# A hybrid decoder layer: inverse blocks by DMA, squares on ACT, pools and output rows in another order

## The chip, the cores and the metric

The kernel runs on one core of a Trainium2 chip. The metric is the time of one execution on the device in microseconds. Five engines work side by side: PE (TensorE: matrix products), DVE (VectorE), ACT (ScalarE), POOL (GpSimd) and SP (SyncE, which here issues nearly all DMAs). Each engine takes its own instructions in the order that was fixed when the program was built; semaphores hold it until what it reads is there.

## The reference

One layer on 1024 tokens of width 1024, all in float32:

- h = LN(x); z = h @ w_in (2304 columns). Of z, 1792 columns belong to time mixing with 8 heads of 64 (r, k, v and three low-rank inputs), 512 to causal pooling with windows 2, 4, 8, 16 and one 128 x 128 product per window.
- Time mixing: z is mixed with the token before it; decay = exp(-exp(-softplus(-u) - 0.5)), a function of one number per element; k is normalised per head; a recurrence over tokens keeps a 64 x 64 state per head; its output is normalised per head, scaled, shifted, gets a bonus and is multiplied by a gate.
- mix = concat(time mixing, pooling) @ w_out; h = LN(alpha h + mix).
- A SwiGLU network (width 2816) and a gated embedding of p follow, and a last LN.

## The kernel before

Products in full precision are made of three rounded ones (high x high, low x high, high x low); the high part is a cast on ACT, the low part a subtraction on DVE. `tile` names buffers in rings (`tag`, `bufs`): a buffer is given again when its last reader is done, in the order of the program text. A scheduler orders each engine's instructions when the program is built: what comes earlier in the text goes first where both could run, and `tc.high_priority()` (around `solve`) lifts a block over all else.

**Order of the work.** Until about 62 us the inputs are loaded, normalised and transposed into `hT`. Then, for a pair index p of heads (4) and a half s of the tokens (2), a tile t = 4 s + p is prepared by `fr(t)` (line 690): `z_pair` makes r, k, v for both halves (s = 0) or `z_again` loads the second half (s = 1), and `front` (line 362) turns them into the operands of the chunked recurrence. Two tiles make a pair, solved by `solve` (line 699): `gram` (line 435) forms the products gB, gK of 64-token chunks; `inverse` (line 462) inverts unit triangular 64 x 64 blocks; `chain` (line 544) walks over 8 chunks, three small products and three short DVE steps each; `post` (line 597) normalises, gates and stores a tile to `ya_d`. The loop at line 707 has `fr(t+2)`, `fr(t+3)`, `solve` of the pair t/2, four times; the pools (lines 712 to 716: `pool_group`, `pool_out`, rows to `yb_d`) follow in the text. When the last pool is done, `zpool` is closed and its memory becomes pool `s4`: `out_weights` (line 727) loads and splits w_out in 16 pieces, `mix(tt)` (line 737) loads and splits a row block of 128 tokens and makes its 2 x 24 products pm. Blocks 0 to 3 need only the first half of the tokens, and run beside the last solves; the rest comes after them. From about 645 us the second half of the layer runs.

**The steps that the change touches.** `front` computes the decay as a polynomial of degree 6 of t1 = tanh: one ACT step (line 379), five DVE steps (line 381), one ACT step into `wx` (line 385). In `inverse` the 16 x 16 diagonal blocks of gB are masked out (dg, line 472), summed to 16 columns (dc, line 474), stored to DRAM by one DMA and loaded in another arrangement, one block per partition, by a second (lines 476, 477); gB loses its diagonal blocks (line 478). After the block inversion on DVE (lines 485 to 511) `ef` holds each inverse and its transpose; one DMA stores both, one loads them back with 16 columns (cc, lines 516, 518), and DVE spreads them with the mask into E_ and F_ (line 521). Then PE multiplies: pn (gB by F_), and three rounds pzz. In `post` the reciprocal root gets one Newton step by three DVE operations (lines 607 to 609).

The queue of SP holds one DMA behind the other: one that waits for a semaphore holds those behind it.

Of the kernel before, what the change touches and what calls it, by code (L numbers as in the profile page):

```python
# [23 lines left out]
NC = 8  # L24
# [6 lines left out]
DECAY = [7.38403150e-01, -2.23932079e-01, 3.39554149e-02, -3.43247040e-03,  # L31
         2.60245296e-04, -1.58445669e-05, 7.95516283e-07]
# [10 lines left out]
def hybrid_layer(ctx, tc, x, pT, w_in, cols, rows, lora, gl, pool_w, w_out,  # L43
# [24 lines left out]
    jm = cq.tile([128, 128], F32, name="jm")  # L68
    V.tensor_scalar(jm, bones, 1.0 / 64, None, ALU.mult)
    cmat = cq.tile([128, 128], F32, name="cmat")  # L70
    V.tensor_tensor(cmat, ident, jm, ALU.subtract)
# [4 lines left out]
    for h in range(2):  # L76
        r = slice(64 * h, 64 * h + 64)
        G.affine_select(out=gmask[r, 0:64], in_=gmask[r, 0:64], pattern=[[1, 64]],
                        compare_op=ALU.is_gt, fill=0.0, base=0, channel_multiplier=-1)
        G.affine_select(out=gmask[r, 64:128], in_=gmask[r, 64:128], pattern=[[1, 64]],  # L80
                        compare_op=ALU.is_ge, fill=0.0, base=0, channel_multiplier=-1)
        G.affine_select(out=bmask[r, :], in_=bmask[r, :], pattern=[[-16, 4]],
                        compare_op=ALU.is_ge, fill=0.0, base=0, channel_multiplier=1)
        G.affine_select(out=bmask[r, :], in_=bmask[r, :], pattern=[[16, 4]],
                        compare_op=ALU.is_ge, fill=0.0, base=15, channel_multiplier=-1)
    e0 = cq.tile([128, 65 * NC + 1], F32, name="e0")
# [9 lines left out]
    qb = cq.tile([128, 2], F32, name="qb")  # L96
    V.memset(qb[:, 0:1], DECAY[5])
    V.memset(qb[:, 1:2], DECAY[0])

# [12 lines left out]
    V.tensor_scalar(oka, col[:, KA:KA + 4], -0.5, 1.0, ALU.mult, ALU.add)  # L112
    lor = cq.tile([128, 512], F32, name="lor")
# [19 lines left out]
    st1 = cp.tile([128, 2, 6], F32, name="st1")  # L133
# [50 lines left out]
    with pa:  # L184
# [74 lines left out]
        def z_mm(j):  # L259
# [102 lines left out]
        def front(pair, q, p, s, r, k, v):  # L362
# [22 lines left out]
            S.activation(wx3[:, :, 1:65], v3(pc), AF.Identity, bias=qb[:, 1:2])  # L385
# [75 lines left out]

        def inverse(pr):
# [5 lines left out]
            for q in range(2):  # L468
                A4 = gB[:, q, :, 0:64].rearrange("p c (q t) -> p c q t", q=4)
                dg = kb("dg")  # L470
                dg4 = dg.rearrange("p c (q t) -> p c q t", q=4)
                V.tensor_tensor(dg4, A4, bmask[:, None, :, None].to_broadcast([128, NC, 4, 16]), ALU.mult)
                dc = s1.tile([128, NC, 16], F32, name="dc", tag="dc", bufs=2)
# [40 lines left out]
            for q in range(2):  # L514
                d2 = dp.tile([2 * NC, 128, 16], F32, name="d2", tag="d2", bufs=4)
                nc.sync.dma_start(d2.rearrange("(x c) (a i) t -> (c a) x (i t)", x=2, i=16), ef[QR[q]])
                cc = s1.tile([128, 2 * NC, 16], F32, name="cc", tag="cc", bufs=2)
                nc.sync.dma_start(cc, d2.rearrange("g p t -> p g t"))
                E_, F_ = [s1.tile([128, NC, 64], F32, name=n, tag=n, bufs=2) for n in ("ex", "fx")]
                for i, t in ((1, F_), (0, E_)):  # L520
                    V.tensor_tensor(t.rearrange("p g (q t) -> p g q t", q=4),
                                    cc[:, NC * i:NC * i + NC, None, :].to_broadcast([128, NC, 4, 16]),
                                    bmask[:, None, :, None].to_broadcast([128, NC, 4, 16]), ALU.mult)
                EF.append((E_, F_))

# [71 lines left out]
        def post(d, py):  # L597
# [4 lines left out]
            S.activation(ys, py, AF.Square)  # L602
            pvv = chp.tile([128, 512], F32, name="pvv", tag="ch")
            mm(pvv, jm, ys, True, True)
# [6 lines left out]
            V.scalar_tensor_tensor(ys, ys, col[:, LG + p:LG + p + 1], d["bv"], ALU.mult, ALU.add)  # L611
            pg = chp.tile([128, 512], F32, name="pgate", tag="ch")
# [26 lines left out]
        def pool_group(g):  # L639
# [5 lines left out]
            pz = z_mm(14 + g)  # L645
# [75 lines left out]
        s4 = ostk.enter_context(tc.tile_pool(name="a4", bufs=2, side="right"))  # L721
        wo = act_tiles("wo")
# [4 lines left out]
        def out_weights():  # L727
            for i in range(8):
                k = OUT_K[i]
                for cf in range(2):  # L730
                    h, l = wo_part(i, cf)
                    r = s4.tile([128, 512], F32, name="wr4", tag="o", bufs=2)
# [4 lines left out]
        def mix(tt):  # L737
# [13 lines left out]
            def part(cf):  # L751
                cs = slice(512 * cf, 512 * cf + 512)
                if tt < 4:
                    o = s4.tile([128, 512], F32, name="o", tag="o", bufs=2)
# [3 lines left out]
                ps = mmp.tile([128, 512], F32, name="pm", tag="mm")  # L758
                for i in range(n):
                    wh, wl = wo_part(i, cf)  # L760
                    mm(ps, yh[i], wh, i == 0, False)
                    mm(ps, yh[i], wl, False, False)
                    mm(ps, yl[i], wh, False, i == n - 1)
                V.tensor_tensor(o, ps, o, ALU.add)  # L764
                if tt < 4:
                    nc.sync.dma_start(m_d[tsl, cs], o)
                    V.bn_stats(st1[:, cf, :], o)
            if tt >= 6:
                return yh, yl
            for cf in range(2):  # L770
                part(cf)
            if tt < 4:
                V.bn_aggr(mv1[:, tt, :], st1.rearrange("p a b -> p (a b)"))

        out_weights()
        for tt in range(4):
            mix(tt)
# [448 lines left out]
```

## Time and profile before

| | |
|---|---|
| median of 3 timed runs | 1352.28 us (1350.77 to 1353.28) |
| the profiled execution | 1357.52 us, span 1355.8 us |
| PE busy | 1309.3 us, 97% of the span |
| DVE busy | 1023.8 us, 76% |
| ACT busy | 526.9 us, 39% |
| granted TensorE clock | 0.990 of full, mean |
| DMA | 117101 packets, 173.52 MB |

Busy times are a union of the instructions' spans; matmuls are pipelined and their ends are modelled, so a busy PE can still be slower than its best. PEclk is the TensorE clock that was granted, as a share of 2.4 GHz.

### The profile page before, as it was taken

Reading aid. Unit: us, or ns where it says so; the run is one execution under the profiler, and the core shown is the slowest. Engines: PE = TensorE matmul, PEld = TensorE weight load, DVE = VectorE, ACT = ScalarE, POOL = GpSimd, SP = SyncE. Lnnn points to the kernel's source line nnn. Section 1 sums busy time; section 2 is a strip of 40 time slices with the busy share of each in tenths; the row PEclk is TensorE's granted clock in tenths of the full one; section 3 lists DMA queues with packets and bytes.
Section 4 is the critical chain, followed back from the end, with each engine's and each line's share of the span. In section 5 each row is a group of like instructions: output and inputs, shape, how many; then the busy total and the mean of one; then the engine's idle time right before and its main releaser. Section 6 shows DMA issues by size and latency. Waiting matters only on the chain.

```text
span 1355.8 us, 22923 instructions
## 1 busy us (share of the span) xinstructions
PE 1309.3 (97%) x9028; PEld 1029.2 (76%) x9028; DVE 1023.8 (76%) x1807; ACT 526.9 (39%) x889; POOL 12.8 (1%) x48
## 2 busy tenths in 40 slices
PE   6999999999997989999999999999999999999997
PEld 5787777777666667778888888888888888887886
DVE  6937566569698884556889989777766767987868
ACT  5823432244334511176434333223333334553530
POOL 0000000000000000000000000000000000000000
PEclk9999999999998999999999999999999999999999
DMA  8621130122123343263433336332323237987803
GB/s 280 216 107 51 55 75 10 59 78 55 41 58 103 91 120 93 102 215 131 150 107 117 114 113 224 116 110 102 101 79 107 101 119 261 319 282 249 264 24 124
DMA packets 117101, 173.52 MB, mean 128 GB/s; under 512 B 34688, under 2 KB 43904, under 8 KB 116992
## 3 DMA queue, kind: packets, MB, share of 16 engines
q1 hardware_dynamic: 116848, 172.01, 38.8%
q8 instruction: 71, 1.16, 0.4%
q14 instruction: 38, 0.31, 0.1%
q10 hardware_dynamic: 144, 0.04, 0.0%
HBM read 124.03 MB, written 47.97 MB: 127 GB/s over the span
## 4 chain that ended last, share of the span: by engine, by line
PE 73%; DVE 14%; DMA 8%; ACT 3%; issue 2%; SPq 0%; DVEq 0%; ACTq 0%
PE p L49 31%; PE pz L49 10%; PE pgt L49 7%; PE py L49 6%; PE pm L49 5%; PE px L49 4%; DMA ar<-a_d 2%; PE pzz L49 1%; PE pg L49 1%; PE cw L49 1%; PE cs L49 1%; DMA ab<-d 1%; DMA wdr<-ff_down 1%; DVE da L830 1%; PE cu L49 1%
## 5 line engine op out<-in xcount | busy, mean ns | idle before, releaser
L49 PE MATMUL p<-tb,p 128*128 128x512 f32 x1056 | 253.0, 395 | 0.0
L49 PEld LDWEIGHTS p<-tb,p 128*128 128x128 f32 x1056 | 198.7, 188 | 47.0
L49 PE MATMUL pz<-hT,wh 128*128 128x512 f32 x576 | 190.9, 406 | 0.0
L49 PE MATMUL p<-h,p 128*128 128x512 f32 x792 | 188.6, 392 | 0.0
L49 PEld LDWEIGHTS p<-h,p 128*128 128x128 f32 x792 | 148.7, 188 | 33.0
L829 ACT CAST p<-a 128x512 fp32r<-128x512 f32 x132 | 81.2, 622 | 181.3 <-PE p L49 138.4
L49 PEld LDWEIGHTS pz<-hT,wh 128*128 128x128 f32 x576 | 107.4, 188 | 32.9 <-issue 4.7
L49 PE MATMUL pz<-hT,wl 128*128 128x512 f32 x288 | 117.5, 408 | 0.0
L830 DVE TENSOR_TENSOR p<-a,p 128x512 fp32r<-128x512 f32 x132 | 89.3, 687 | 12.5 <-ACT p L829 12.1
L49 PE MATMUL pm<-wo,mh 128*128 128x512 f32 x224 | 78.6, 418 | 3.3 <-DVE o L764 1.4
L1001 DVE TENSOR_TENSOR u<-p,u 128x512 f32<-128x512 f32 x66 | 45.3, 687 | 31.6 <-PE p L49 31.6
L49 PEld LDWEIGHTS pz<-hT,wl 128*128 128x128 f32 x288 | 54.1, 188 | 16.5 <-issue 3.8
L49 PE MATMUL px<-da 128*128 128x512 f32 x276 | 64.3, 390 | 0.0
L49 PEld LDWEIGHTS px<-da 128*128 128x128 f32 x276 | 51.8, 188 | 10.9
L49 PEld LDWEIGHTS pm<-wo,mh 128*128 128x128 f32 x224 | 41.3, 188 | 15.8 <-ACT wo L734 1.9
L245 DVE TENSOR_TENSOR wl<-wr,wh 128x512 fp32r<-128x512 f32 x36 | 24.7, 688 | 35.1 <-ACT wh L243 34.3
L49 PE MATMUL pgt<-wg,h 128*128 128x512 f32 x192 | 48.4, 396 | 0.0
L49 PE MATMUL py<-da 128*128 128x512 f32 x204 | 47.7, 389 | 0.0
L49 PE MATMUL pm<-wo,ml 128*128 128x512 f32 x112 | 46.6, 419 | 0.0
L49 PEld LDWEIGHTS py<-da 128*128 128x128 f32 x204 | 38.3, 188 | 8.1
L243 ACT CAST wh<-wr 128x512 fp32r<-128x512 f32 x36 | 22.3, 619 | 56.3 <-PE pz L49 31.8
L1022 DVE TENSOR_TENSOR gs<-p,u 128x512 f32<-128x512 f32 x44 | 30.4, 690 | 18.1 <-PE p L49 17.3
(325 smaller groups left out, 2351.0 us busy)
## 6 DMA issues: line engine op xcount, KB each, us to landing
ar<-a_d SPq DMA_DIRECT2D x77, 256.0 KB, 4.2
wdr<-ff_down SPq DMA_DIRECT2D x55, 256.0 KB, 3.8
a<-ff_gate SPq DMA_DIRECT2D x44, 256.0 KB, 2.8
a<-ff_up SPq DMA_DIRECT2D x44, 256.0 KB, 2.8
a_d<-s SPq DMA_DIRECT2D x44, 256.0 KB, 2.3
b<-ff_down SPq DMA_DIRECT2D x22, 512.0 KB, 5.8
wr<-w_in SPq DMA_DIRECT2D x36, 256.0 KB, 2.8
a_d<-gs SPq DMA_DIRECT2D x33, 256.0 KB, 2.2
```

The lines of the kernel that those rows point to most:

```text
L49: PE.matmul(o, lhsT=l, rhs=r, start=a, stop=z)
L243: S.copy(wh, wr)
L245: V.tensor_tensor(wl, wr, wh.bitcast(F32), ALU.subtract)
L829: S.copy(h, r)
L830: V.tensor_tensor(l, r, h.bitcast(F32), ALU.subtract)
L1001: V.tensor_tensor(t, ps, u, ALU.add)
L1022: V.tensor_tensor(d, ps, u, ALU.add)
```

## The change

In `front` the polynomial is written as a product of squares: ACT makes (t1 + b0) squared, (t1 + b1) squared plus a constant, and (t1 + b2) squared; two DVE steps multiply them; ACT scales into `wx`. In `post` y0 squared is made on ACT and two DVE steps remain (the constant of the Newton step goes into the scale of the squares and `hlg`); the gate product of the last two tiles uses another PSUM bank. In `inverse` gB is stored to DRAM with rows of 64 and a pitch that makes the four diagonal blocks of a 64 x 64 matrix one strided pattern; the blocks are loaded from it. On the way back, the inverses are stored as diagonal blocks into DRAM buffers that were filled with zeros at the beginning, and E_ and F_ are loaded from these whole. gB's diagonal blocks are cleared by one multiplication with a mask. Pools are put before `fr(6)` and `fr(7)` in the text; the last pool's z products go half by half; row blocks are loaded two at a time ahead of the weights; weights come by column halves, in four buffers; the products of a part are sorted: all high x high, all low x high, all high x low. Setup lines (masks, constants) change with it and are left out here.

```diff
 front:
             pc = k2("pc")
-            S.activation(pc, t1, AF.Identity, scale=DECAY[6], bias=qb[:, 0:1])
-            for n in (0.0, DECAY[4], DECAY[3], DECAY[2], DECAY[1]):
-                V.scalar_tensor_tensor(pc, pc, n, t1, ALU.add, ALU.mult)
+            pd = k2("pd")
+            S.activation(pc, t1, AF.Square, bias=qb[:, 0:1])
+            S.activation(pd, t1, AF.Square, bias=qb[:, 1:2])
+            S.activation(pd, pd, AF.Identity, bias=qb[:, 3:4])
+            S.activation(t1, t1, AF.Square, bias=qb[:, 2:3])
+            V.scalar_tensor_tensor(pc, pc, QE[0], pd, ALU.add, ALU.mult)
+            V.scalar_tensor_tensor(pc, t1, QE[2], pc, ALU.add, ALU.mult)
...
 before inverse:
+        HS = 64 * 64 + 64
+        def rows_of(d, h):
+            return d.rearrange("(c h r) -> c h r", c=NC, h=2)[:, h, 0:64 * 64].rearrange("c (p t) -> p c t", t=64)
+        def blocks_of(d):
+            return d.rearrange("(g r) -> g r", g=64)[:, 0:1024].rearrange("g (s t) -> g s t", t=64)[:, :, 0:16]
+        d2 = [[dp.tile([2 * NC * HS], F32, name=f"d2{q}{x}", bufs=1) for x in range(2)] for q in range(2)]
+        zt = s1.tile([128, 2 * NC * HS // 128], F32, name="zt", tag="k2", bufs=KA_BUFS)
+        G.memset(zt, 0.0)
+        for q in range(2):
+            for x in range(2):
+                nc.scalar.dma_start(d2[q][x].rearrange("(p r) -> p r", p=128), zt)
 inverse:
             for q in range(2):
-                V.tensor_tensor(dg4, A4, bmask[:, None, :, None].to_broadcast([128, NC, 4, 16]), ALU.mult)
-                V.tensor_reduce(dc, dg.rearrange("p c (q t) -> p c t q", q=4), AX.X, ALU.add)
-                d1 = dp.tile([NC, 128, 16], F32, name="d1", tag="d1", bufs=4)
-                nc.sync.dma_start(d1.rearrange("c p t -> p c t"), dc)
-                nc.sync.dma_start(abf[QR[q], 0:256], d1.rearrange("c (a s) t -> (c a) (s t)", a=8))
-                V.tensor_tensor(gB[:, q, :, 0:64], gB[:, q, :, 0:64], dg, ALU.subtract)
+                d1 = dp.tile([2 * NC * HS], F32, name="d1", tag="d1", bufs=4)
+                for h, R in enumerate(HR):
+                    nc.sync.dma_start(rows_of(d1, h), gB[R, q, :, 0:64])
+                nc.sync.dma_start(abf[QR[q], 0:256].rearrange("g (s t) -> g s t", t=16), blocks_of(d1))
...
             for q in range(2):
-                nc.sync.dma_start(d2.rearrange("(x c) (a i) t -> (c a) x (i t)", x=2, i=16), ef[QR[q]])
-                nc.sync.dma_start(cc, d2.rearrange("g p t -> p g t"))
-                for i, t in ((1, F_), (0, E_)):
-                    V.tensor_tensor(t..., cc..., bmask..., ALU.mult)
+            for i in (1, 0):
+                for q in range(2):
+                    nc.sync.dma_start(blocks_of(d2[q][i]), ef[QR[q], i, :].rearrange("g (i t) -> g i t", t=16))
+                for q in range(2):
+                    for h, R in enumerate(HR):
+                        nc.sync.dma_start(EF[q][i][R], rows_of(d2[q][i], h))
+            for q in range(2):
+                V.tensor_tensor(gB[:, q, :, 0:64], gB[:, q, :, 0:64],
+                                omask[:, None, :].to_broadcast([128, NC, 64]), ALU.mult)
 post:
-            V.scalar_tensor_tensor(ys, pvv, GN_EPS, y0, ALU.add, ALU.mult)
-            V.scalar_tensor_tensor(ys, ys, -0.5, y0, ALU.mult, ALU.mult)
-            V.scalar_tensor_tensor(y0, ys, 1.5, y0, ALU.add, ALU.mult)
+            S.activation(ys, y0, AF.Square)
+            V.scalar_tensor_tensor(ys, pvv, GN_EPS, ys, ALU.add, ALU.mult)
+            V.scalar_tensor_tensor(y0, ys, 3.0, y0, ALU.subtract, ALU.mult)
...
-            pg = chp.tile([128, 512], F32, name="pgate", tag="ch")
+            pg = psa("pgate") if s and p > 1 else chp.tile([128, 512], F32, name="pgate", tag="ch")
 z_mm:
-            for q in range(2):
-                for hf in range(2):
+            for a in range(2):
+                for b in range(2):
+                    q, hf = (b, a) if by_half else (a, b)
                     z_part(pz[hf], w, q, hf)
 pool_group:
-            pz = z_mm(14 + g)
+            pz = z_mm(14 + g, g == 0)
 the loop over pairs:
+        pools = []
         for t in range(0, 8, 2):
+            for g in ({4: (3, 2, 1, 0)}).get(t, ()):
+                pools.append(pool_group(g))
+                if len(pools) > 1:
+                    pool_out(g + 1, *pools[-2])
+                if g == 0:
+                    pool_out(0, *pools[-1])
             if t < 6:
...
-        pools = [pool_group(3)]
-        for g in (2, 1, 0):
-            pools.append(pool_group(g))
-            pool_out(g + 1, *pools[-2])
-        pool_out(0, *pools[-1])
 out_weights (tags "o" get 4 buffers instead of 2, here and in mix):
-            for i in range(8):
-                k = OUT_K[i]
-                for cf in range(2):
+            for cf in range(2):
+                for i in range(8):
+                    k = OUT_K[i]
 mix, part(cf):
+                w = [wo_part(i, cf) for i in range(n)]
                 for i in range(n):
-                    wh, wl = wo_part(i, cf)
-                    mm(ps, yh[i], wh, i == 0, False)
-                    mm(ps, yh[i], wl, False, False)
-                    mm(ps, yl[i], wh, False, i == n - 1)
+                    mm(ps, yh[i], w[i][0], i == 0, False)
+                for i in range(n):
+                    mm(ps, yl[i], w[i][0], False, False)
+                for i in range(n):
+                    mm(ps, yh[i], w[i][1], False, i == n - 1)
 rows 0 to 3:
-        out_weights()
-        for tt in range(4):
-            mix(tt)
+        for t2 in (0, 2):
+            rows_ = [mix(t2), mix(t2 + 1)]
+            if t2 == 0:
+                out_weights()
+            for cf in range(2):
+                for part in rows_:
+                    part(cf)
...
```

## Rows read from the trace of the kernel before

**Rows 1.** The page's first part: busy time and share of the span of each engine.
```profile
PE 1309.3 (97%) x9028; PEld 1029.2 (76%) x9028; DVE 1023.8 (76%) x1807; ACT 526.9 (39%) x889; POOL 12.8 (1%) x48
```
**Rows 2.** Busy time by stage; last columns: granted clock, DMA share, GB/s.
```profile
core 0: us, PE busy (x) PEld busy (x) DVE busy (x) ACT busy (x) POOL busy (x), PEclk, DMA share, GB/s
0.00:41.00 41.00, 29.52 (x128) 21.98 (x129) 28.34 (x82) 26.28 (x43) 2.83 (x18) 1.00 0.86 286
...
62.00:124.00 62.00, 61.78 (x258) 47.80 (x256) 36.16 (x53) 23.43 (x40) 1.29 (x3) 1.00 0.23 85
124.00:288.00 164.00, 162.09 (x1600) 121.97 (x1600) 98.76 (x189) 54.19 (x95) 1.89 (x7) 0.98 0.19 56
288.00:415.00 127.00, 116.92 (x1516) 84.43 (x1514) 111.44 (x226) 52.00 (x87) 5.82 (x18) 0.98 0.22 56
415.00:428.00 13.00, 10.80 (x243) 10.01 (x244) 9.31 (x17) 7.16 (x11) 0.63 (x1) 0.67 0.46 118
428.00:500.00 72.00, 66.92 (x940) 47.63 (x937) 63.48 (x130) 29.29 (x54) 0.31 (x2) 1.00 0.32 93
500.00:560.00 60.00, 58.17 (x846) 43.97 (x845) 29.82 (x68) 9.26 (x22) 0.00 (x0) 1.00 0.31 87
...
645.00:1124.00 479.00, 479.00 (x2072) 388.98 (x2071) 385.96 (x611) 162.34 (x270) 0.00 (x0) 1.00 0.36 119
```
**Rows 3.** Waits of PE in 124 to 600 us: total, times, longest.
```profile
PE pn L49 <- DVE fx L521: 6.8, 4, 2.1
PE pp L49 <- issue: 3.1, 1, 3.1
...
PE pg L49 <- DVE bk L417: 1.4, 2, 0.7
...
```
**Rows 4.** Groups by line: shapes, count, busy us, mean ns, idle before.
```profile
L381 DVE SCALAR_TENSOR_TENSOR pc<-pc,t 128x512 f32<-128x512 f32 x40 | 27.4, 686 | 10.8 <-ACT pc L379 10.3
...
L474 DVE TENSOR_REDUCE dc<-dg 128x128 f32<-128x512 f32 x8 | 8.2, 1029 | 0.0
...
L379 ACT ACTIVATE pc<-t,qb 128x512 f32<-128x512 f32 x8 | 5.7, 710 | 0.0
L521 DVE TENSOR_TENSOR fx<-cc,bmask 128x512 f32<-128x512 f32 x8 | 5.5, 688 | 3.3 <-DMA cc<-d 3.3
...
L472 DVE TENSOR_TENSOR dg<-gB,bmask 128x512 f32<-128x512 f32 x8 | 5.5, 683 | 0.0
```
**Rows 5.** DVE in order of time, third pair: start us, us.
```profile
390.49 0.68 DVE L449 TENSOR_TENSOR gB<-pg,gmask 128x512 f32<-128x512 f32 x1
...
400.49 0.17 DVE L490 TENSOR_TENSOR tm<-ef,ab 128x4 f32<-128x4 f32 x1 [0.98 <-DMA ab<-d]
...
409.61 0.37 DVE L512 COPY ef<-ef 128x256 f32<-128x256 f32 x1
```
**Rows 6.** DMA issues: count, KB each, median us from issue to landing.
```profile
d<-ef SPq DMA_DIRECT2D x8, 128.0 KB, 2.4
cc<-d SPq DMA_DIRECT2D x8, 128.0 KB, 3.4
...
d<-dc SPq DMA_DIRECT2D x8, 64.0 KB, 2.4
ab<-d SPq DMA_DIRECT2D x8, 64.0 KB, 2.1
```
**Rows 7.** PE in order of time between pools and output products; in brackets: stood.
```profile
411.48 1.10 PE L49 MATMUL pp<-wsa,plw 128*128 128x512 f32 x2 [3.09 <-issue]
413.51 2.04 PE L49 MATMUL pp<-wsa,plw 128*128 128x512 f32 x2 [0.93 <-DVE wsa L673]
417.65 3.68 PE L49 MATMUL pn<-fx,gB 64*64 64x64 f32 x64 [2.10 <-DVE fx L521]
...
428.51 0.51 PE L49 MATMUL pm<-wo,mh 128*128 128x512 f32 x1
```
**Rows 8.** SP in the same stretch: issue of the first row's second half.
```profile
437.07 0.38 SPq L746 DMA_DIRECT2D mr<-ya_d  x1
```

More of the change, by code (lines that the diff above doesn't have):

```diff
@@ L29 @@
 GN_EPS = 1e-5 * 64
-DECAY = [7.38403150e-01, -2.23932079e-01, 3.39554149e-02, -3.43247040e-03,
-         2.60245296e-04, -1.58445669e-05, 7.95516283e-07]
+QB = [2.6446236909266547, -4.777402204072105, -7.825890616949517]
+QE = [148.19110777287312, 64.07475031771858, 7.586255131509925]
+QS = 7.95516283e-07
 MU, W0, A0, KK, KA, RK, LG, LB, PS, IG, IB, MG, MB = 0, 14, 18, 22, 26, 30, 34, 38, 42, 46, 54, 62, 70
@@ L67, in hybrid_layer @@
     V.memset(bones[64:128, 64:128], 1.0)
-    jm = cq.tile([128, 128], F32, name="jm")
-    V.tensor_scalar(jm, bones, 1.0 / 64, None, ALU.mult)
     cmat = cq.tile([128, 128], F32, name="cmat")
-    V.tensor_tensor(cmat, ident, jm, ALU.subtract)
+    V.scalar_tensor_tensor(cmat, bones, -1.0 / 64, ident, ALU.mult, ALU.add)
     gmask = cq.tile([128, 128], F32, name="gmask")
@@ L85, in hybrid_layer @@
                         compare_op=ALU.is_ge, fill=0.0, base=15, channel_multiplier=-1)
+    omask = cq.tile([128, 64], F32, name="omask")
+    V.tensor_scalar(omask.rearrange("p (q t) -> p q t", q=4), bmask[:, :, None].to_broadcast([128, 4, 16]),
+                    -1.0, 1.0, ALU.mult, ALU.add)
     e0 = cq.tile([128, 65 * NC + 1], F32, name="e0")
@@ L95, in hybrid_layer @@
     V.memset(epsg, GN_EPS)
-    qb = cq.tile([128, 2], F32, name="qb")
-    V.memset(qb[:, 0:1], DECAY[5])
-    V.memset(qb[:, 1:2], DECAY[0])
+    qb = cq.tile([128, 4], F32, name="qb")
+    for i, c in enumerate(QB + [QE[1]]):
+        V.memset(qb[:, i:i + 1], c)
     col = cp.tile([128, NCOL], F32, name="col")
@@ L112, in hybrid_layer @@
     V.tensor_scalar(oka, col[:, KA:KA + 4], -0.5, 1.0, ALU.mult, ALU.add)
+    hlg = cq.tile([128, 4], F32, name="hlg")
+    V.tensor_scalar(hlg, col[:, LG:LG + 4], -0.5, None, ALU.mult)
     lor = cq.tile([128, 512], F32, name="lor")
@@ L130, in hybrid_layer @@
     hT = act_tiles("hT")
-    st1 = cp.tile([128, 2, 6], F32, name="st1")
+    st1 = cp.tile([128, 4, 2, 6], F32, name="st1")
     mv1 = cp.tile([128, 4, 2], F32, name="mv1")
@@ L257, in z_part, with z_mm @@
                 mm(pz, ls[q][:, i, :], hh[:, k, :], False, k == KT - 1)
[L259 removed]
+        def z_mm(j, by_half=False):
             w = z_weights(j)
             pz = [mmp.tile([128, 512], F32, name=f"pz{hf}", tag="mm") for hf in range(2)]
[L262 to L263 removed]
+            for a in range(2):
+                for b in range(2):
+                    q, hf = (b, a) if by_half else (a, b)
                     z_part(pz[hf], w, q, hf)
@@ L384, in front @@
             wx3 = wx[:, 0:65 * NC].rearrange("p (c t) -> p c t", t=65)
-            S.activation(wx3[:, :, 1:65], v3(pc), AF.Identity, bias=qb[:, 1:2])
+            S.activation(wx3[:, :, 1:65], v3(pc), AF.Copy, scale=QS)
             Ep = s2.tile([128, NC, 65], F32, name="Ep", tag="ep", bufs=1)
@@ L721, in hybrid_layer @@
         s4 = ostk.enter_context(tc.tile_pool(name="a4", bufs=2, side="right"))
+        OB = 4
         wo = act_tiles("wo")
@@ L727, in out_weights @@
         def out_weights():
-            for i in range(8):
-                k = OUT_K[i]
-                for cf in range(2):
+            for cf in range(2):
+                for i in range(8):
+                    k = OUT_K[i]
                     h, l = wo_part(i, cf)
-                    r = s4.tile([128, 512], F32, name="wr4", tag="o", bufs=2)
+                    r = s4.tile([128, 512], F32, name="wr4", tag="o", bufs=OB)
                     nc.sync.dma_start(r, w_out[128 * k:128 * k + 128, 512 * cf:512 * cf + 512])
@@ L753, in part @@
                 if tt < 4:
-                    o = s4.tile([128, 512], F32, name="o", tag="o", bufs=2)
+                    o = s4.tile([128, 512], F32, name="o", tag="o", bufs=OB)
                     nc.sync.dma_start(o, h_d[tsl, cs])
@@ L766, in part @@
                     nc.sync.dma_start(m_d[tsl, cs], o)
-                    V.bn_stats(st1[:, cf, :], o)
+                    V.bn_stats(st1[:, tt, cf, :], o)
             if tt >= 6:
                 return yh, yl
+            if tt < 4:
+                return part
             for cf in range(2):
                 part(cf)
-            if tt < 4:
-                V.bn_aggr(mv1[:, tt, :], st1.rearrange("p a b -> p (a b)"))
-        out_weights()
-        for tt in range(4):
-            mix(tt)
+        for t2 in (0, 2):
[5 more added lines that the diff above has]
+                    part(cf)
+            for tt in (t2, t2 + 1):
+                V.bn_aggr(mv1[:, tt, :], st1[:, tt].rearrange("p a b -> p (a b)"))
     sp = ctx.enter_context(tc.tile_pool(name="b", bufs=2, reuse_waits="tile"))
```

15 lines of the change are left out of this document (3 added, 12 removed).

## The prediction

> **What bounds the kernel now.** I read the busy line of the page first: PE is busy 97% of the span, VectorE (DVE) 76% [rows 1]. The reader is to see that this is no proof of a kernel that can't get faster: it is a mean over stages. So the second view was the busy time by stage [rows 2]. From 645 to 1124 us PE is busy in every microsecond at full clock, 2072 matmuls in 479.0 us, 0.231 us each; nothing of the change is there. From 124 to 560 us, where the time mixing is solved, the rows differ: PE stands still 1.9 us in 124–288, 10.1 in 288–415, 2.2 in 415–428, 5.1 in 428–500 and 1.8 in 500–560, together 21.1 us. The granted clock of the same rows is 0.98, 0.98, 0.67, 1.00 and 1.00. With two levels, 1.2 and 2.4 GHz, that is (0.02×164 + 0.02×127 + 0.33×13)/0.5 = about 20 us at the lower one, and half of it, 10 us, is lost wherever PE had work. So 31 us can be seen to be recoverable. In 288–415 and 428–500 DVE is busy 111.4 of 127 and 63.5 of 72 us: there it nearly sets the pace; in 500–560 it is busy 29.8 of 60. The third view, the waits of PE in 124–600, says who held it: the product pn of the inverse waits for fx in each of the four pairs (6.8 us), the pooling product pp for 3.1 + 0.9 us, pg for bk 1.4 us [rows 3]. The low clock comes behind such stands: in the row 415–428, right after those of the hand-over below [rows 2, 7].
>
> **The change part by part.** Sums are made against the profiled execution, 1357.5 us (span 1355.8); the median of the timed runs, 1352.3, lies 5.2 below it, and I take the same difference off at the end.
>
> *Squares on ACT.* Eight fronts lose three of five DVE steps of the decay polynomial: 24 × 0.686 = 16.5 us of DVE; each gains three ACT steps (four instead of one): 24 × 0.71 = 17.0 us of ACT at the price of the step that is there [rows 4]. In post one of three 0.68 us DVE steps goes to ACT, eight times: DVE −5.5, ACT +5.7 at that price. ACT is busy 52.0 of 127 us in 288–415 and 29.3 of 72 in 428–500 [rows 2], so this hides; without that cover it would cost at most 23 us spread over eight tiles. The latency of one front falls: five DVE steps one after the other were 3.4 us; now three ACT steps (2.1) precede the first of two DVE steps (1.4).
>
> *Inverse blocks by DMA.* Per tile, eight tiles: the mask product dg, the reduction dc (1.03), the subtraction, and the two mask products fx and ex go: 0.68 + 1.03 + 0.68 + 2 × 0.69 = 3.77 us of DVE; one masking product of the same shape as dg comes in (0.68), issued where DVE waits for the blocks anyway. Net −3.1 × 8 = −24.7 us [rows 4]. With the two items above DVE loses 46.7 us of 1023.8.
>
> Entry of the inverse, read on the third pair: the last gB eviction ends at 391.17, the first step on the blocks starts at 400.49, 9.3 us later, with dg, dc and two DMA hops between [rows 5]. After the change the hops follow the eviction directly: two half stores (256-byte rows, 64 partitions each; no such transfer in the trace) and one block load of 64-byte pieces. I bound a hop by the nearest rows, 2.1 us (ab from d) and 3.4 (cc from d, 2048 pieces of 64 bytes); d from dc, also in 64-byte pieces, takes 2.4 [rows 6]. An issue holds SP for 0.38 us [rows 8]. So 0.4 + 2 × 2.1 = 4.6 to 0.4 + 2 × 3.4 = 7.2 us: 2.1 to 4.7 saved; I take 3.4, hops near 2.7.
>
> Exit: the copy of the inverse ends at 409.98, pn starts at 417.65, 7.7 us later [rows 5, 7]. After: one store hop (2.4 is the row of d from ef), one load hop in two halves, no mask product: 0.1 + 2.4 + 0.4 + 2.1 = 5.0 to 0.1 + 2 × 3.4 + 0.4 = 7.3. Saved 0.4 to 2.7; I take 1.6. Together 5.0 us a pair (2.5 to 7.4). SP issues 18 DMAs a pair instead of 8, ten more at 0.38: 3.8 us a pair. Queued behind them in SP's order are the row and weight loads, which feed products that PE has 0.231 us for; I take +1 in all (0 to +4). The second set, E, is needed only after pn (3.7 us) [rows 7] and may come behind F in SP's order.
>
> The Trainium skill (DMA: Bandwidth & Descriptors, Rules for kernel authors) speaks against this part: it says that two transfers to disjoint partition halves serialize, and asks for one transfer over 128 partitions. By that rule each hop with halves would stand at its upper bound, the pair would gain 2.5 instead of 5.0 us, and the sum below would be some 2 us less; no row of before has a pair of halves.
>
> The four fills with zeros (4 × 266 KB) are issued from ACT. Their tile comes in the ring of k2 tiles behind those of the flips, so I put them into the stage 62–124, where the DMA share is 0.23. At the 286 GB/s of 0–41 us they take 3.7 us of all engines: 0 if they run beside the products, +3.7 if a load on the path waits; I take 0 [rows 2].
>
> *Pools earlier, rows ahead of weights, rounded products first, halves of the last pool tile.* Between the last z products and the first output product PE does two pool outputs and the small products of the third inverse: it stands 3.09, 0.93 and 2.10 us, then runs pn and pzz at the low clock, and pm starts at 428.51 [rows 7]. The pool ops stand behind the seventh front (t = 6) in priority now; the change puts them ahead. The loads of rows come in ahead of the weights: the second half of the first row (mr from ya_d) is issued only at 437.07 in SP's order [rows 8], although it needs nothing new. With the rounded products first, 16 of a part's 24 need only ACT's casts and not DVE's remainder; and four buffers instead of two keep more weight loads in flight. By halves, half of the last tile's 24 + 24 products (12 × 2 × 0.231 = 5.5 us) ends before the other begins, so its copy and sums start up to 2.8 us earlier. What is late next: the yb_d store and the row load, two hops of 2.1 to 3.4 us that nothing shortens.
>
> **The sum in PE time.** A shorter solve gains only where PE stood or ran slow.
> - Hand-over 407–428: 6.1 us of stands and 0.33 × 13 = 4.3 us of clock, 10.4 in all; I take −7 (0 to −10.4), since two hops stay.
> - The other three stands at pn: 6.8 − 2.1 = 4.7, and the clock in 124–288 and 288–415, (3.3 + 2.5) = 5.8; 10.5 in all. Each engine's order is fixed when the program is built, and a shorter path is answered by an earlier place for pn, so I take a third, −3.5 (from −10.5; upward see the second rival).
> - 428–500: 5.1 us. DVE loses here 3 × 0.686 of a front, twice dg, dc and the subtraction, and two post steps: 2.1 + 4.8 + 1.4 = 8.3 of its 63.5 us. I take −3.5 (0 to −5.1).
> - Stands elsewhere in 124–560 (21.1 − 6.1 − 4.7 − 5.1 = 5.2) and waits inside the chain of small products, where short DVE copies queue behind fewer long ones: −2.5 (0 to −8).
> - SP's added issues +1; ACT's added steps +0.5 (0 to +3).
>
> Total −15: 1342.5 for the profiled execution, 1337 for the median. A measurement of this kernel can tell 0.2%, 2.7 us, from no change.
>
> **Rivals.**
> 1. *The fill only moves.* PE had z and pm products to run beside the solves, so shorter solves let them end later instead; and the hand-over stays as long, because the output stage can't open before the last pool row is stored. For it: 97% busy, and in 500–560 only 1.8 us of stands to win. Against it: the clock of 0.67 and the 6.1 us of stands in one place. Half the hand-over and none of the rest: −5, 1347.
> 2. *Slower: PE stands longer at pn.* The exit's loads are now four per set in SP's order, 256-byte rows in halves. If both hops come at 3.4 us and SP holds the loads by another 3 us, while the order on PE expects them early, the stand at pn goes from 1.7 to 6 us, four times: +17, and the clock falls behind each, +3. With the −11.5 of the other terms: +8.5, 1361. It decides from about 3 us more than today's 1.7 at each pn. For it: PE already waits there in every pair, and the loads share SP with 256 KB weight loads. Against it: as many hops as before, and two mask products fewer.
> 3. *Larger.* The solves set the end of this stretch, and everything seen is won: −30, 1322. For it: DVE's 88% in two windows. Against it: PE has the same work.
>
> By the Trainium skill (DMA: Bandwidth & Descriptors, Issuing engines are not separate DMA queues) transfers issued from ACT share the 16 engines with SP's, so the zeros would cost their 3.7 us wherever DMA is the limit; the DMA share of 0.23 says it is not there, and the sum stays.
>
> **How the numbers follow.** Forecast 0.60 (own range 1327 to 1345), fill only moves 0.17, slower 0.13, larger 0.10. Below 1318 (every term at its lower end) 4 in 100, above 1357 12 in 100: range 1318 to 1357. Faster by over 0.2%: all of the forecast and the larger case, most of the first rival, 0.81; within 0.2%: the rest of that and the mild part of the second, 0.06; slower 0.13.
>
> **What would show it.** Right: pm's first product before 420 us; no window near the hand-over with a clock of 0.67; DVE's busy time near 977 us; eviction to first block step under 7.5 us; copy to pn under 7 us; the solves' end some 15 us earlier, everything from the gate products on shifted by that. Wrong: waits of pn for the loads above 5 us a pair; low clock in new places; output products that wait for rows behind SP's new DMAs; or unchanged gaps with fewer DVE steps, which would say that DVE was never in the way.

## The result: 1.3% slower, where 1.1% faster was forecast

Timed side by side, the changed kernel takes 1371.95 us (median, 1368.89 to 1374.69) and the kernel before 1352.78: a ratio of 1.0130 (95% interval 1.0110 to 1.0151). The sign is wrong, and the time lies above the range. The profiled execution is 1369.88 us (span 1368.1), 12.4 more than that of before. The first product of the network (pgt) comes 17.1 us later, at 618.3 instead of 601.2 us; 4.8 us of that are regained behind it. So the loss arises before 618 us.

The page's first part after the change, the row that answers to [rows 1]:

```profile
PE 1318.6 (96%) x9028; PEld 1026.7 (75%) x9028; DVE 983.6 (72%) x1746; ACT 544.7 (40%) x921; POOL 14.6 (1%) x49
```

DVE is relieved by 40.2 us, nearly the 46.7 forecast, and the kernel is slower. Busy time by stage (columns as in [rows 2]; the last row is a stage of its own):

```profile
124.00:288.00 164.00, 162.69 (x1612) 121.60 (x1612) 86.33 (x170) 61.75 (x108) 2.88 (x8) 1.00 0.23 65
288.00:415.00 127.00, 120.34 (x1518) 83.44 (x1516) 97.07 (x203) 61.47 (x105) 6.44 (x16) 0.99 0.31 81
415.00:428.00 13.00, 4.94 (x7) 1.83 (x7) 12.04 (x24) 3.95 (x7) 0.55 (x3) 0.53 0.49 98
428.00:500.00 72.00, 67.59 (x966) 47.78 (x966) 43.28 (x87) 26.82 (x50) 0.20 (x1) 0.92 0.34 98
500.00:560.00 60.00, 59.95 (x795) 45.69 (x796) 31.55 (x73) 9.78 (x20) 0.00 (x0) 1.00 0.37 95
560.00:600.00 40.00, 33.00 (x340) 23.73 (x337) 15.57 (x39) 7.31 (x16) 0.00 (x0) 0.91 0.25 85
```

From 124 to 415 us PE is fuller than before and its clock better. Then come two holes: 4.94 us of work in the 13 us of 415–428 at a granted clock of 0.53 (nearly all at 1.2 GHz; before 10.80 at 0.67), and 33.00 of 40 us in 560–600, where before had:

```profile
560.00:600.00 40.00, 37.72 (x175) 29.48 (x174) 20.86 (x39) 19.95 (x31) 0.00 (x0) 1.00 0.54 190
```

The waits of PE in 124–600 us (total, times, longest):

```profile
PE pm L51 <- ACT mh L772: 7.6, 2, 7.1
PE pm L51 <- DVE ys L636: 6.3, 1, 6.3
PE pbo L51 <- DVE rb L431: 4.4, 2, 2.7
```

pn, the place of my slower rival, is not among them: its 6.8 us of [rows 3] are gone, and the price stands at other products. What happened at pn is seen on SP and on PE, at the second pair. SP in order of time (start, us, count), before, then after:

```profile
321.07 1.29 SPq L516 DMA_DIRECT2D d<-ef  x2
323.51 1.41 SPq L518 DMA_DIRECT2D cc<-d  x2
```

```profile
320.32 2.75 SPq L540 DMA_DIRECT2D d<-ef  x4
323.17 0.62 SPq L543 DMA_DIRECT2D ex<-d  x1
323.88 2.62 SPq L543 DMA_DIRECT2D fx<-d  x4
326.56 1.99 SPq L543 DMA_DIRECT2D ex<-d  x3
```

One issue of these loads and stores holds SP for 0.6 to 0.7 us, not for the 0.38 us of [rows 8]. From the first to the last of the loads back there were 1.4 us, part of it waiting; now the eight issues take 5.2, and the stores 2.75 instead of 1.3, one after the other. PE in the same stretch, before, then after (the numbers behind the names are the shapes):

```profile
327.20 3.22 PE L49 MATMUL pn<-fx,gB 64*64 64x64 f32 x64 [1.99 <-DVE fx L521]
330.21 2.56 PE L49 MATMUL pzz<-ex,fx 64*64 64x64 f32 x64
332.64 4.47 PE L49 MATMUL pzz<-rr,fx 64*64 64x64 f32 x128
```

```profile
328.68 0.33 PE L51 MATMUL pn<-fx,gB 64*64 64x64 f32 x2
328.94 0.73 PE L51 MATMUL pz<-hT,wh 128*128 128x512 f32 x2
...
332.50 0.32 PE L51 MATMUL pn<-fx,gB 64*64 64x64 f32 x2
332.75 0.50 PE L51 MATMUL pz<-hT,wl 128*128 128x512 f32 x1
...
333.42 0.33 PE L51 MATMUL pzz<-ex,fx 64*64 64x64 f32 x2
...
336.76 1.14 PE L51 MATMUL pzz<-ex,fx 64*64 64x64 f32 x30
...
345.38 1.15 PE L51 MATMUL pzz<-rr,fx 64*64 64x64 f32 x32
```

The order, fixed when the program is built, now has large products between the first pn and the last pzz: 24, 21, 6 and 27 in the four pairs instead of 3, 0, 0 and 1 (the trace's records have 5 for the 6). PE hardly stands there (1.7 us in all, for DVE's rr); it uses up its fill (the z, pool and output products that it has to run beside the solves) early, and the inverse ends later. Nor does the trace show PE late for the loads: the last of them landed at 331.25 us, 2.2 us before the first pzz that reads E starts. In the four pairs it landed 3.5, 2.2, 4.8 and 0.3 us before that product. From the copy of the inverse to the last pzz the pairs take 25.1, 25.8, 28.7 and 24.8 us, together 104.4; before 20.7, 16.1, 18.6 and 18.2, together 73.6. That sum, S below, is the number to watch.

The fill is missed in the third pair. PE from 410 us, and once more at the end of the last solve:

```profile
410.25 2.01 PE L51 MATMUL pm<-wo,mh 128*128 128x512 f32 x4 [0.52 <-issue]
419.40 1.22 PE L51 MATMUL pm<-wo,mh 128*128 128x512 f32 x2 [7.15 <-ACT mh L772]
...
425.27 2.07 PE L51 MATMUL pbo<-rb,bones 128*128 128x512 f32 x2 [2.65 <-DVE rb L431]
...
591.08 1.22 PE L51 MATMUL pm<-wo,mh 128*128 128x512 f32 x2 [6.25 <-DVE ys L636]
```

The output products start at 410.25 instead of 428.51 us, as forecast, but after four of them nothing is ready: the z products and pools are done (last pool product 394.8, before 415.6 us) and the inverse is late.

### The profile page after: what moved, and what is told of

The parts are those of the page before. It is cut to its first block, busy times and chain, and to the rows that moved or that the text cites. A ratio compares the mean times of both kernels' runs of the same rounds, so it can differ in the third digit from the quotient of the medians.

```text
span 1368.1 us, 22962 instructions
## 1 busy us (share of the span) xinstructions
PE 1318.6 (96%) x9028; PEld 1026.7 (75%) x9028; DVE 983.6 (72%) x1746; ACT 544.7 (40%) x921; POOL 14.6 (1%) x49
## 4 chain that ended last, share of the span: by engine, by line
PE 87%; DVE 6%; ACT 3%; DMA 2%; issue 1%; SPq 0%; DVEq 0%; ACTq 0%
PE p L51 31%; PE pz L51 12%; PE py L51 8%; PE px L51 8%; PE pm L51 7%; PE pgt L51 7%; PE pg L51 2%; PE pzz L51 2%; PE cw L51 1%; PE cs L51 1%; PE pe L51 1%; PE pn L51 1%; PE cu L51 1%; PE pbo L51 1%; PE pt L174 1%
## 5 line engine op out<-in xcount | busy, mean ns | idle before, releaser
L862 ACT CAST p<-a 128x512 fp32r<-128x512 f32 x132 | 81.1, 622 | 176.9 <-PE p L51 131.4
L51 PE MATMUL pm<-wo,mh 128*128 128x512 f32 x224 | 75.0, 438 | 14.8 <-ACT mh L772 7.6
L1034 DVE TENSOR_TENSOR u<-p,u 128x512 f32<-128x512 f32 x66 | 45.2, 686 | 30.3 <-PE p L51 30.2
L1055 DVE TENSOR_TENSOR gs<-p,u 128x512 f32<-128x512 f32 x44 | 30.3, 689 | 17.6 <-PE p L51 16.5
L51 PEld LDWEIGHTS pgt<-wg,h 128*128 128x128 f32 x192 | 35.6, 188 | 8.3
```

The costliest lines, as they stand in the source:

```text
L51: PE.matmul(o, lhsT=l, rhs=r, start=a, stop=z)
L862: S.copy(h, r)
L1034: V.tensor_tensor(t, ps, u, ALU.add)
L1055: V.tensor_tensor(d, ps, u, ALU.add)
```

## Experiments

Each ratio compares a kernel's times with those of the kernel before on the same chip, with its 95% interval; it can differ a little from the quotient of the medians.

**Which part loses: the change less one part.** `e1`, whole change, both ways of the inverse as before (weight buffers 3 and dc buffers 1, for space):

```diff
-                for h, R in enumerate(HR):
-                    nc.sync.dma_start(rows_of(d1, h), gB[R, q, :, 0:64])
+                V.tensor_tensor(dg4, A4, bmask[:, None, :, None].to_broadcast([128, NC, 4, 16]), ALU.mult)
...
-        OB = 4
+        OB = 3
```

> The changed kernel with the inverse's blocks moved as before (mask, reduce, one store and one load each way); one buffer less for weights (3 instead of 4) and one for dc, since memory is short. Theory A (the inverse by DMA costs: twelve issues of about 0.65 us on SP on the way back, in halves, so pn and pzz stretch and the fill is used up inside the solves): from the copy of the inverse to the last pzz 16 to 21 us as before instead of 25 to 29, no stretch at low clock of over 10 us behind 400 us, 1335 to 1352. Theory B (pools ahead of the fronts use up the fill, whatever the inverse does): the hole at 400 to 440 stays, 1362 to 1375. Theory C (the output stage with rows in pairs ahead of weights starves PE): the 7 us stands of pm stay, 1360 or more.

Measured 1355.05 us, 1.0016 (1.0002 to 1.0029), 3 us above the range of theory A, S 72.2: nearly all of the loss goes with the inverse. `e2` is the kernel before with the inverse's part alone:

```diff
-                nc.sync.dma_start(cc, d2.rearrange("g p t -> p g t"))
+                    for h, R in enumerate(HR):
+                        nc.sync.dma_start(EF[q][i][R], rows_of(d2[q][i], h))
```

> The kernel before with only the inverse's blocks by DMA. Theory A: the exit from copy to last pzz is 24 to 29 us in each pair, 1360 to 1372. Theory B and C: DVE loses 25 us and nothing else happens, 1343 to 1354.

1365.21, 1.0090 (1.0070 to 1.0109), S 98.2: the part alone makes most of the loss. `e3` traces the pools last, `e4` has the output stage of before:

```diff
-            for g in ({4: (3, 2, 1, 0)}).get(t, ()):
-                pools.append(pool_group(g))
...
+        pools = [pool_group(3)]
```

> The changed kernel with the pools traced after the last solve, as before. Theory B: the z products lie in 390 to 410 again, the hole closes, 1345 to 1356. Theory A: exit times stay 25 to 29 us, 1363 to 1373; the hole only moves. Theory C: 1363 or more with stands of pm.

```diff
-        for t2 in (0, 2):
-            rows_ = [mix(t2), mix(t2 + 1)]
+        out_weights()
+        for tt in range(4):
+            mix(tt)
```

> The changed kernel with the output stage as before (rows one at a time behind the weights, two buffers, products in threes). Theory C: the 7.6 us stand of pm behind its row's cast and the 6.9 us stand at 584 go, 1350 to 1360. Theory A or B: the fill is missing for another reason, 1366 to 1378.

1366.78, 1.0106 (1.0086 to 1.0126), and 1365.82, 1.0090 (1.0075 to 1.0106); S 100.4 and 99.9, e4 just under the 1366 that A and B gave it. Neither is the cause; by the ratios each stands for 3 to 5 of the 18 us, and for e3 the interval overlaps that of the whole change.

**One part in the kernel before.** `e5` only the way back by DMA, `e6` only the way in (the stores of gB and the block loads, and the mask product on gB), `e7` only the squares and the gate's bank, `e8` squares, output stage and tile by halves (weight buffers 3):

```diff
 e5:
+                    for h, R in enumerate(HR):
+                        nc.sync.dma_start(EF[q][i][R], rows_of(d2[q][i], h))
 e6:
+                for h, R in enumerate(HR):
+                    nc.sync.dma_start(rows_of(d1, h), gB[R, q, :, 0:64])
+                nc.sync.dma_start(abf[QR[q], 0:256].rearrange("g (s t) -> g s t", t=16), blocks_of(d1))
 e7, e8:
+            S.activation(pc, t1, AF.Square, bias=qb[:, 0:1])
 e8:
+            rows_ = [mix(t2), mix(t2 + 1)]
```

> The kernel before with only the way back changed (four stores of diagonal blocks, eight loads of E and F halves; entry with mask and reduction as before). Theory A1 (the twelve issues on SP and the late E stretch the solve): pn to last pzz 16 to 20 us instead of 10 to 14 in each pair, all of the loss of the whole inverse part: 1360 to 1370. Theory A2 (the entry costs: whole gB rows through DRAM, and the DVE time it frees lets a front run into the block steps): 1346 to 1356.

> The kernel before with only the entry changed (gB rows stored whole, blocks loaded from them, one mask product instead of mask, reduction and subtraction; the way back as before). Theory A1: 10 us of DVE work less and nothing lost, 1340 to 1352, eviction to first block step 6 to 8.5 us. Theory A2: 1358 to 1368, with a stand of PE of over 5 us near 410 us behind a front's pbo.

> The kernel before with only the squares on ACT (polynomial and Newton step) and the gate product's bank. My forecast's term: DVE loses 22 us, ACT gains 23, the end 2 to 6 us earlier, 1346 to 1351. Rival: ACT's longer queue delays casts and copies behind it, 1352 to 1358.

> The changed kernel with pools at the end and the inverse as before (three weight buffers, one for dc): squares, halves and the output stage. If pools ahead of the fronts cost what the run with the inverse as before still lost (its seventh front's scan came at 425.5 instead of 413.3 us), this is 1342 to 1350 with that scan near 410; if the output stage or the squares cost it, 1352 to 1357.

Measured: e5 1368.16, 1.0108 (1.0081 to 1.0135), S 99.9; e6 1345.55, **0.9943 (0.9922 to 0.9963)**, S 69.3; e7 1351.05, 0.9982 (0.9969 to 0.9996); e8 1350.64, 0.9975 (0.9959 to 0.9991), between the ranges of its two theories. The two halves of the inverse's part have opposite signs: the way in gains some 8 us, the way back loses 15.

**Why the way back loses.** `e9` is e5 with the second half of each load issued from ACT's queue; `e12` the whole change with the way back of before (weight buffers 3):

```diff
 e9:
-                        nc.sync.dma_start(EF[q][i][R], rows_of(d2[q][i], h))
+                        (nc.scalar if h else nc.sync).dma_start(EF[q][i][R], rows_of(d2[q][i], h))
 e12:
+                nc.sync.dma_start(cc, d2.rearrange("g p t -> p g t"))
```

> Only the way back changed, as in the exit-only run, but the second half of each load of E and F is issued from ACT's queue and not from SP's. In the order that PE gets, 7, 3, 3 and 2 large products now stand between the first pn and the last pzz of the four pairs, where the exit-only kernel has 22, 24, 5 and 27 and the kernel before 3, 0, 0 and 1. Theory S (eight loads one after the other on one queue, in fact and in the plan, are the price): pn to last pzz back to 10 to 14 us, the last E lands 2 to 3 us earlier, 1350 to 1361. Theory P (the hops and the small pieces are the price, on whichever queue): loads still land late, PE stands at pn and pzz instead of running fill, 1364 to 1372.

> The changed kernel with nothing but the way back as before (three weight buffers). If the way back is the whole loss: 1340 to 1347, no slower than the same with pools at the end. If pools ahead of the fronts cost by themselves, as the first run with the inverse as before hints: 4 to 6 us more than with pools at the end, 1345 to 1352, the seventh front's scan some 12 us later.

e9: 1353.52, 1.0001 (0.9990 to 1.0012), S 74.7. The same bytes, packets and zeros, and the loss is gone. One sign of theory S failed: the last E landed 9.9 us after the copy of the inverse (mean of four pairs), in e5 10.4, so 0.5 us earlier and not 2 to 3.

e12: 1353.45, 1.0008 (0.9995 to 1.0021), S 69.6, above both of its ranges: all the rest together costs nothing and gains nothing. Next the line of e9 in the whole change (`e13`), in the inverse alone (`e16`, e2 with that line), and the reverse, issues without their contents, in the kernel before (`e15`):

```diff
 e13, e16:
-                        nc.sync.dma_start(EF[q][i][R], rows_of(d2[q][i], h))
+                        (nc.scalar if h else nc.sync).dma_start(EF[q][i][R], rows_of(d2[q][i], h))
 e15, ahead of the load of cc:
+                dm = s1.tile([128, NC, 16], F32, name="dm", tag="dc", bufs=2)
+                for j in range(4):
+                    R, k = QR[j % 2], slice(8 * (j // 2), 8 * (j // 2) + 8)
+                    nc.sync.dma_start(dm[R, :, k], d2[0:NC, R, k].rearrange("g p t -> p g t"))
```

> The whole change, but the second half of each of the loads E and F is issued from ACT's queue instead of SP's. Theory S (the loss of 19 us is the time that SP takes to issue eight loads per pair one after the other): as with the way back of before, 1353.45 us, so 1350 to 1357 us; pools and first output products stay early, and the large products that PE has between the first pn and the last pzz fall from 24, 21, 6, 27 to 7, 3, 1, 2. Rival P (in the whole change the loss comes from pools and rows being early and the way back only triggers it): the time stays above 1362 us.

> The kernel before with nothing changed but four loads added ahead of each of the two loads of cc on SP's queue, 64 partitions x 8 pieces of 32 bytes each, from the buffer that was just stored, into memory that nobody reads. Theory S (issue time on SP alone is the price): SP issues eight more loads per pair, 0.6 us each, 4 to 5 us before fx can be made; slower, 1359 to 1368 us, and pn and pzz of a pair take longer from first to last than the 9.7 to 14.0 us of before in the pairs where the order puts large products between them (planned 6, 17, 2, 9). Rival C (what costs is what the loads carry, whole rows with zeros into E and F, 141357 packets instead of 117101): within 3 us of before, 1350 to 1356 us.

> The kernel before with both ways of the inverse by DMA, the second half of each of the loads E and F from ACT's queue; nothing else of the change. Theory S: the way in alone gave 1345.55, the way back from two queues 1353.5 us, no loss; together 1344 to 1351 us. If the parts don't add for a reason of their own (rival O of the run before): 1351 to 1357 us. If the way back still costs beside the way in: above 1358 us.

e13: 1351.35, 0.9981 (0.9968 to 0.9994), S 74.1; one word in one line takes some 20 us off the changed kernel. e16: 1344.97, **0.9939 (0.9919 to 0.9960)**, S 73.2, the fastest version found, level with e6, and 20 us faster than e2. e15: 1365.98, 1.0104 (1.0076 to 1.0132), S 87.9. SP in e15 at the second pair:

```profile
322.56 2.63 SPq L520 DMA_DIRECT2D dm<-d  x4
325.23 0.62 SPq L522 DMA_DIRECT2D cc<-d  x1
325.95 3.31 SPq L520 DMA_DIRECT2D dm<-d  x4
329.30 0.62 SPq L522 DMA_DIRECT2D cc<-d  x1
```

Eight loads that nobody reads, issued on SP ahead of those that count, cost as much as the whole way back (e5, 1.0108). Here the load that counts is late: the second cc landed 12.6 us after the copy (mean of four pairs), before 7.3. The traced execution, 1359.71 us, is the fastest of four, 6 us below their median.

So the eight loads in a row on SP's queue are the cause, from both sides: with half of them on ACT's queue the loss is gone in three kernels (e9, e13, e16), and added alone they lose as much. By what way they cost in the changed kernel is another question, and the traces of it and of e13 go against the plain answer, late data. Landing times in e13, then its PE at the second pair:

```profile
ex<-d ACTq DMA_DIRECT2D x8, 128.0 KB, 4.1
ex<-d SPq DMA_DIRECT2D x8, 128.0 KB, 4.4
fx<-d ACTq DMA_DIRECT2D x8, 128.0 KB, 4.5
fx<-d SPq DMA_DIRECT2D x8, 128.0 KB, 4.9
```

```profile
326.83 3.35 PE L51 MATMUL pn<-fx,gB 64*64 64x64 f32 x64 [2.33 <-DMA fx<-d]
329.97 2.36 PE L51 MATMUL pzz<-ex,fx 64*64 64x64 f32 x64
332.26 0.50 PE L51 MATMUL pz<-hT,wh 128*128 128x512 f32 x1
...
336.63 1.15 PE L51 MATMUL pzz<-rr,fx 64*64 64x64 f32 x32
```

From two queues each load lands later after its issue (4.1 to 4.9 us instead of 3.5), which eats most of what the shorter row of issues saves. Means of four pairs, from the copy on: the last E landed after 10.8 us in the changed kernel and 10.1 in e13, and pn began after 8.0 us in both. What differs is the order: the large products between the first pn and the last pzz, counted from start to start, hold PE for 24.8 us in the four pairs of the changed kernel, 5.7 in e13 and 2.1 in the kernel before. In e13 PE even stands for the loads, 8.2 us ahead of the third pair's pn (9.6 in e16), and is faster all the same. Thus the queue is shown as the cause, and of the 30.3 us by which S is longer than in e13, 19.1 are these products. No run keeps PE's order and changes only the queue, so what the order costs by itself is not shown. Why the scheduler orders so isn't in a trace; that it counts the issues of one queue one after the other would fit.

**Why the gains don't add.** `e10` way in, squares, output stage and tile by halves (weight buffers 3); `e11` way in and squares; `e14` e11 with the pools ahead in the text; `e17` e13 with the output stage and the pool tile of before:

```diff
 e14, against e11:
+            for g in ({4: (3, 2, 1, 0)}).get(t, ()):
+                pools.append(pool_group(g))
 e17, against e13:
-            pz = z_mm(14 + g, g == 0)
+            pz = z_mm(14 + g)
...
-        for t2 in (0, 2):
-            rows_ = [mix(t2), mix(t2 + 1)]
+        for tt in range(4):
+            mix(tt)
```

> Entry by DMA, squares on ACT, halves and the new output stage; way back as before and pools at the end (three weight buffers). If the parts add as they did alone (entry -7.9, squares and output -2.8): 1340 to 1345. If they share one stand (PE at the third pair): 1344 to 1349.

> Entry by DMA and squares on ACT alone, rest as before. Adding up -7.9 and -2.4: 1341 to 1346; if the output stage is what helps beside the entry, 1345 to 1350 and slower than the run with it.

> The kernel before with the way in by DMA, the squares on ACT and the pools ahead of fr(6) in the text; the output stage, the tile by halves and the way back are those of before. Theory F (way in and squares alone gave -7.9 and -2.4 us but together +1.2 because the seventh front then goes ahead of the pools: the last pool product is at 438.4 instead of 403.0 us, the first output product at 448.7 instead of 419.0): with the pools early again the parts add, 1341 to 1347 us, first output product before 425 us. Rival O (the two parts win the same stands, which can be won once only, and the place of the pools does not matter): 1350 to 1356 us, though the first output product is early.

> The whole change with the loads back from two queues (1351.35 us), but the output stage (rows two at a time, weights by column halves, four buffers, sorted products) and the pool tile by halves are those of before. Two readings of what keeps the whole change from the 1345 us of the inverse alone: theory M (the output stage in its new order costs: its rows and weights lie later against the last solves): 1341 to 1348 us, near 1344.97 (inverse alone) and 1347.36 (way in, squares, pools). Rival Q (squares and early pools use up what the inverse wins, whatever the output stage does): 1349 to 1354 us.

e10: 1355.60, 1.0023 (1.0013 to 1.0032); e11: 1354.21, 1.0012 (0.9997 to 1.0027); both missed, though their S is the smallest of all (63.5 and 66.2). PE in e11:

```profile
417.69 2.08 PE L51 MATMUL pbo<-rb,bones 128*128 128x512 f32 x2 [8.65 <-DVE rb L430]
420.52 1.76 PE L51 MATMUL pn<-fx,gB 64*64 64x64 f32 x28 [0.75 <-DVE fx L534]
...
437.28 1.12 PE L51 MATMUL pp<-wsa,plw 128*128 128x512 f32 x2
```

In this order the seventh front is ahead of the last pool: PE stands 8.65 us for that front's rb, and the last pool product, which opens the output stage, is at 437.28. In e14 the pools are ahead:

```profile
405.76 1.12 PE L51 MATMUL pp<-wsa,plw 128*128 128x512 f32 x2
411.47 3.38 PE L51 MATMUL pn<-fx,gB 64*64 64x64 f32 x64 [0.28 <-DVE fx L534]
419.62 0.49 PE L51 MATMUL pm<-wo,mh 128*128 128x512 f32 x1
```

e14: 1347.36, 0.9952 (0.9936 to 0.9968), just above the 1341 to 1347 expected, so most of what e11 misses was this order. The squares then add nothing to the way in (e6, 0.9943). e17 missed both of its theories: 1356.65, 1.0012 (1.0000 to 1.0024), 5 us above e13 though only the output stage and the pool tile by halves differ in the text. Its S is 81.1: the order has nine large products in the inverse of the fourth pair, where e13 has two. So the output stage of the change is not what keeps e13 at 1351.

## Why the prediction was wrong

- **The step that failed** is the exit of the inverse: "0.1 + 2.4 + 0.4 + 2.1 = 5.0 to 0.1 + 2 × 3.4 + 0.4 = 7.3. Saved 0.4 to 2.7; I take 1.6", with "ten more at 0.38: 3.8 us a pair ... I take +1 in all (0 to +4)". Up to pn nothing was saved: both halves of the first F had landed 7.4 us after the copy (mean of four pairs), where before it was ready, mask product included, after 7.2. The hops took 2.7 us for the store and 3.5 for the load (rows below), at or above the upper ends, 2.4 as the row and 3.4 as the bound. The 0.38 us was the row of a plain load of a row block; these loads, 64 partitions by 8 rows of 256 bytes, hold SP for 0.57 to 0.68 us, the stores about as long, and twelve of them stand in a row instead of four. Copy to pn, forecast to fall from 7.3 to 5.7 us (mean of four), is 8.0. The larger miss is a term that the sum doesn't have: it ends at pn, puts the queue's cost on other loads behind it, and takes the stretch from pn to the last pzz as it was. That stretch went from 11.1 to 18.2 us a pair, by the large products that the order now has in it; copy to the last pzz rises by 7.7 us a pair.

```profile
d<-gB SPq DMA_DIRECT2D x16, 128.0 KB, 2.7
ex<-d SPq DMA_DIRECT2D x16, 128.0 KB, 3.5
fx<-d SPq DMA_DIRECT2D x16, 128.0 KB, 3.5
d<-zt ACTq DMA_DIRECT2D x4, 260.0 KB, 3.1
...
d<-ef SPq DMA_DIRECT2D x16, 64.0 KB, 2.7
...
ab<-d SPq DMA_DIRECT2D x8, 64.0 KB, 3.3
```

- **The slower rival** had the place (loads held by SP) and too small a price (1361), but the wrong sign of its symptom: it looked for a stand at pn. "A shorter path is answered by an earlier place for pn", I wrote; here the answer was more fill among pn and pzz, and it is paid where the fill ends, at 412–428 and 585–591 us. "The second set, E, ... may come behind F" holds for the data: E is ready 10.8 instead of 9.0 us after the copy, but in the second pair it lies there from 331.25 us on and pzz starts at 333.4 (before 330.2).
- **Entry** (2.1 to 4.7 us a pair, 3.4 taken): eviction to first block step takes 7.4, 7.7, 8.6 and 7.7 us; before 7.3, 8.4, 9.3 and 9.2. It gains 0.7 us on the mean, since the hops are longer (2.7 and 3.3 us, rows above; 2.4 and 2.1 in [rows 6]). Alone it is worth 8 us all the same (e6); that DVE's 3.1 us less per tile bring this is argued, not shown.
- **Squares** (the three steps at DVE's and ACT's price): each ACT step is 0.71 to 0.72 us, DVE fell, and it hides (e7, −2.4 us). "ACT's added steps +0.5" holds.
- **Hand-over** ("I take −7"): pm starts at 410.25, before the 420 asked for, yet the window at its end has the clock of 0.53. The stands moved from pp to pm. Beside the squares, output stage and halves change nothing (e7, e8).
- **Zeros**: issued from ACT at 63.5 to 64.9 us, 3.1 us each; POOL alone waited for them, once for 9.3 us, and 0 was right as far as that shows.
- **DVE as the bound**: relief of 40 us moved nothing by itself. My sum added terms as if each stand could be won alone; e10, e11 and e17 show that they are not additive.

The Trainium skill (DMA: Bandwidth & Descriptors, Rules for kernel authors) says of two transfers to disjoint partition halves that they serialize, and I had charged it 2 us, as longer hops. On one queue a half lands hardly later than the whole cc (3.5 against 3.4 us, [rows 6]); from two queues, in e13, it takes 4.1 to 4.9 us, which agrees with the page. The same page (Issuing engines are not separate DMA queues) says that several issuing engines save only the sequencer's time to start a transfer, "which is usually small relative to the DMA itself". The trace agrees as far as the data go: in e13 the last load landed 0.7 us earlier after the copy than in the changed kernel. The 20 us that e13 gains are far more than that.

**What stays open.** Above S of about 85 all kernels lose 12 to 19 us; between 63 and 75 they lie from 1345 to 1356 us, and S does not order them. Part of that is the place of the seventh front against the pools (e11, e14); the rest, such as why the whole change with two queues stays 6 us above the inverse alone, is not settled. Each edit, however small, gives the engines another fixed order, and an effect of 5 us that only one kernel shows can't be put down to its edit.

## What to carry to other kernels

Count the DMAs that a serial path issues in a row on one queue, and price each by a row of the same access pattern; here halves on one queue cost more than the work they saved, and a second queue gave it back. Where an engine is kept full by a fixed order, a longer path need not show as a stand at its place: measure the latency of the step (from its input to its last product), set the landing of its data beside the start of the product that reads them, and look for the price where the fill runs out. If the data lie there before the product starts, it is the order that holds it. Test the parts of a change one by one; here a part worth −8 us hid behind one worth +15.

## What the runs showed of the hardware

The issue of a plain block (wr from w_in, k or v into rkv_d) held SP for 0.33 us where it stood alone, and for 0.56 us right behind the eight loads (rows below). That of a load with 64 partitions by 8 pieces took 0.57 to 0.68 us with pieces of 256 bytes; in e15, with 32 bytes, it took 0.63 us in the median, so there the price didn't go with the bytes. The whole cc, 128 partitions by 16 pieces, took 0.62 us each time in e15, but before, where SP had waited ahead of it, 0.38 to 0.46 us five times and 1.2 to 1.5 us three times. So the price depends on what stands ahead in the queue as well as on the pattern, and these runs don't separate the two. Eight such issues in a row ahead of it let the second cc of e15 land 5.2 us later. SP in the changed kernel, first pair:

```profile
190.35 0.33 SPq L648 DMA_DIRECT2D rkv_d<-k  x1
...
197.24 1.98 SPq L543 DMA_DIRECT2D ex<-d  x3
199.33 0.56 SPq L648 DMA_DIRECT2D rkv_d<-v  x1
```
